# The other order of a block's projections, and scores within 32 tokens on four strips of partitions

## The chip, the cores and the metric

The kernel runs on one core of one Trainium2 chip. A core has a matrix engine (PE, whose weight loads are listed apart as PEld), a vector engine (DVE), an activation engine (ACT), a general engine (POOL) and a queue engine (SP) that issues the DMA transfers. Each works through a list of its own, in the list's order, and the program has it wait on semaphores where it needs another engine's result. The metric is the device time of the whole program in microseconds (us), lower is better. Times are medians of repeated runs on one chip.

## The reference

One layer of a hybrid backbone over 4096 latent tokens of 1024 channels, with a prefix of 256 context tokens:

```python
a_lat = rmsnorm(h_lat, norm_g) * (1.0 + sc_l) + sh_l
q, zf, zb, v, ga, u, ug, gb = split(a_lat @ w_in)            # 8 groups of 512 columns
f = lb + (1 - lb) * sigmoid(z);  k = 1 - f                   # forget gates, forward and backward
S_t = diag(f_t) S_{t-1} + k_t v_t^T;  o_t = S_t^T q_t        # 4 heads of 128, both directions
y = silu(layernorm(depthwise_conv31(u * sigmoid(ug)) + b))   # half the channels along rows, half along columns
h = h_lat + gt * concat(head_rmsnorm(o) * silu(ga), y * silu(gb)) @ w_out
out = rmsnorm(h)
```

The latent scans of both directions start from the final states of the context. All of it is float32; the kernel takes each float32 projection as three float16 products (a high and a low half of each operand, without low times low).

## The kernel before, in words

A first sweep goes forward over 16 blocks of 256 tokens (two groups of 128), a second one goes backward over the groups. The first sweep does the projections of z (both directions), q, v, u and ug, the forward recurrence, the row convolution, and stores what the second sweep needs. The second sweep does the gates ga and gb, the column convolution, the backward state's term, the norms and the output projection.

Inside a block the recurrence of a group (`hgrn`, L707) is done without a loop over tokens. Two tokens s and t belong to the level h (1, 2, 4, ...) where s xor t lies in [h, 2h). For each level, ACT gathers the decayed keys of both directions into a tile `km` (L743), PE multiplies them with the decayed queries into a PSUM tile `pl` (`scores`, L712 to L719), DVE multiplies the keys and queries in the tile `X` by the forget factors of the next level (L750, L751), and a predicated copy under a mask (L754) puts the level's entries of `pl` into the tile `SD`. Level 0 (`kap`, L730) is the token with itself. Levels 1 to 32 are done within halves of 64 tokens: each product has 64 keys as weights and 64 queries as moving columns, the first half on partitions 0 to 63 of the output, the second on 64 to 127. So a level has 16 products (2 groups, 4 heads, 2 halves), and as float32 each is two weight loads and two matmul instructions (passes). The last level, 64, multiplies one half with the other (L761, L762). After it the keys are split into halves of float16 (`split_keys`: `K` on ACT L554 and DVE L555) and transposed by DMA (`X<-K`, L556); with them PE forms the state's increment `pu` (L572), and with the assembled score tile `SC` (ACT copies, L783, L784) the output `po` (L789, L790).

Beside the recurrence of block b run, side by side, the row convolution of b on DVE (`row_conv`, 62 instructions, L690 and L698), the projections, the norm and transposition of the rows of block b + 2 (`prep_rows`), and in blocks 1 to 10 the preparation of the second sweep's weights. `merge` (L46) issues the steps of these generators at an even pace; then a scheduler of the framework, which works with its own estimates of time, settles the order of each engine's list. In the kernel before, the projections beside block b are in this order: ug and u of block b (`project_uv`), v of block b, then z and q of block b + 1 (`project_fq`). The row convolution needs the product `gu` of u and sigmoid(ug), so its generator first idles for a fifth of its steps.

Tiles come from pools with a fixed number of buffers per tag: `X` has 2 (one per group), `km` 3 (shared with `kap`, `SC` and `sg`), the projections' PSUM tile 2, `gu` three tags in turn.

Of the kernel before, what the change touches and what calls it, by code (L numbers as in the profile page):

```python
# [19 lines left out]
P = 128  # L20
# [12 lines left out]
LEVELS = (1, 2, 4, 8, 16, 32)  # L33
# [3 lines left out]
# row packing of the per-channel vectors  # L37
# [5 lines left out]
def merge(*gens):  # L43
    """Issue the steps of several generators side by side, each at an even pace."""
# [28 lines left out]
def rsqrt(nc, pool, out, v, n, tag, eng=None):  # L73
    """out = v ** -0.5 for [128, n] columns, by Newton's iteration to float32's accuracy."""
# [23 lines left out]
def hymba_block(  # L98
# [47 lines left out]
    def exponent(out_s, out_r, ssq):  # L146
        """From a sum of squares: r = a power of two over sqrt(ssq / 2), s = 2^14 / r."""
# [4 lines left out]
        # the halved biased exponent, taken as a number, is 2^-64 of the power sought  # L152
# [7 lines left out]
    def group_scale(ssq, g):  # L160
        """The scale of a group of columns, from sums of its squares."""
# [14 lines left out]
    def split_chunk(hi, lo, st, g, dve=False):  # L176
        """hi + lo = scale * st, both float16."""
# [10 lines left out]
    # ---------------------------------------------------------------- sweep 1  # L188
    wp = ctx.enter_context(tc.tile_pool(name="wp", bufs=1))
    e1 = ctx.enter_context(tc.tile_pool(name="e1", bufs=1))  # L190
    with ExitStack() as s1:
# [55 lines left out]
        def prep_rows(r0, aT):  # L247
            """The same for later blocks: modulated as rows, and transposed by DMA."""
# [28 lines left out]
        def proj_cm(ps, w, aT, ct):  # L277
            """ps[:, j] = columns ct + j of a group, channels on partitions."""
# [38 lines left out]
        masks = m1.tile([P, len(LEVELS), H], U8, name="masks")  # L317
# [3 lines left out]
        # ---------------------------------------------------------- set-up  # L321
        # Staging of what set-up reads: tiles that the blocks use only later.
# [75 lines left out]
        # per-partition columns of the vectors  # L398
# [4 lines left out]
        # silu(c) as c * sigmoid(c); the softmax of two logits as a sigmoid of their difference  # L403
# [5 lines left out]
        # modulation  # L409
        mcol = const([P, 16, 2], name="mcol")  # L410
        for j in MOD:
# [17 lines left out]
            # four rows of 128 at a time, each on a quarter of the columns  # L429
# [18 lines left out]
        with tc.high_priority():  # L448
# [4 lines left out]
            # a normed row of 1024 has no entry over 32, so a^2 <= 2 (1024 g^2 + sh^2)  # L453
# [747 lines left out]
```

## Time and profile before

| what | us |
|---|---|
| median of 3 runs (2247.38 to 2247.63) | 2247.4 |
| span of the profiled execution, from its first to its last instruction | 2247.5 |
| PE busy | 2134.2 |
| PEld busy | 1678.9 |
| DVE busy | 1795.7 |
| ACT busy | 970.8 |
| POOL busy | 462.2 |

The profiled execution's span and the median of the runs differ by 0.1 us, so the trace may be read as the time itself. Busy time is the union of an engine's instructions; matmuls overlap each other, so the length of a matmul is not what it adds: that is the distance from its start to the next one's start. In the timeline a row stands for a run of equal instructions, with its start, its length and its count; the length contains the last instruction's latency, and the next row's start tells what the run really took. A block of the first sweep is seen best between two copies of line 734, of which there is one per block.

### The profile page before, as it was taken

The numbers are of one execution on the slowest core, as the hardware profiler recorded it, in microseconds if no ns is written. First come the engines' busy times: TensorE is split into PE (matmuls) and PEld (weight loads), VectorE is DVE, ScalarE is ACT, GpSimd is POOL, SyncE is SP. The second block draws the span as 40 slices with busy tenths as digits, with TensorE's granted clock in tenths as the row PEclk, the third lists the DMA queues.
The fourth block names the chain that finished last, engine by engine and source line by source line (L and its number), as shares of the span: only waits on it lengthen the run. The fifth ranks groups of instructions, "written<-read, shape, count | busy, mean of one in ns | idle before, by whom it ended". The sixth has DMA issues, their size and how long they took to land. (4 is left out here: it accounts for less than half of the span.)

```text
span 2247.5 us, 47494 instructions
## 1 busy us (share of the span) xinstructions
PE 2134.2 (95%) x18750; PEld 1678.9 (75%) x18750; DVE 1795.7 (80%) x4288; ACT 970.8 (43%) x2150; POOL 462.2 (21%) x1146
## 2 busy tenths in 40 slices
PE   6999999999998999999999999999899999999997
PEld 3778778778777778778778778686667777667776
DVE  5999887887886987987977976988878888877754
ACT  5944535435535435435435434332433333334333
POOL 1120101001010001001101000034444333443332
PEclk8999999999999999999999999999999999999999
DMA  9425435424425345244223205543233232223332
GB/s 363 130 77 165 127 86 156 97 70 137 102 64 164 79 134 166 65 139 109 60 64 77 57 25 160 157 163 108 94 101 101 90 115 97 90 95 105 108 102 71
DMA packets 221448, 251.19 MB, mean 112 GB/s; under 512 B 143812, under 2 KB 147736, under 8 KB 216744
## 3 DMA queue, kind: packets, MB, share of 16 engines
q1 hardware_dynamic: 220104, 239.67, 36.1%
q0 software_dynamic: 1120, 8.49, 1.0%
q8 instruction: 147, 2.41, 0.5%
q14 instruction: 77, 0.63, 0.1%
HBM read 137.99 MB, written 76.55 MB: 95 GB/s over the span
## 5 line engine op out<-in xcount | busy, mean ns | idle before, releaser
L283 PEld LDWEIGHTS <-w 128*128 128x128 f16 x4704 | 451.2, 98 | 67.9 <-issue 2.6
L698 DVE SCALAR_TENSOR_TENSOR yr<-gu,convw,yr 128x224 f32<-128x224 f32 (+2 forms) x900 | 353.1, 442 | 0.0
L1020 DVE SCALAR_TENSOR_TENSOR ycs<-gu_all,convw,ycs 128x256 f32<-128x256 f32 (+2 forms) x828 | 344.2, 467 | 0.0
L283 PEld LDWEIGHTS <-pair 128*128 128x128 f16 x3168 | 308.9, 98 | 36.7
L1118 PE MATMUL py<-wo,yh 128*128 128x512 f32 x1024 | 277.7, 410 | 3.5 <-ACT yh L1102 3.4
L80 POOL TENSOR_SCALAR xqh<-xssq 128x1 f32<-128x1 f32 x30 | 14.9, 498 | 1056.5 <-DVE xssq L256 1056.5
L743 ACT COPY km<-X 128x512 f32<-128x512 f32 x192 | 126.5, 665 | 239.9 <-DVE X L751 236.7
L1118 PEld LDWEIGHTS py<-wo,yh 128*128 128x128 f32 x1024 | 187.3, 190 | 43.3 <-ACT yh L1102 4.4
L987 PE MATMUL ps_gb<-aT,w 128*128 128x256 f16 x1536 | 190.4, 273 | 0.0
L283 PE MATMUL ps_z<-aT,w 128*128 128x256 f16 x1632 | 186.9, 274 | 1.9 <-DVE aT L241 1.4
L294 PE MATMUL pv<-w,aT 128*128 128x512 f16 x816 | 184.1, 379 | 0.1
L975 PE MATMUL ps_ga<-w,aT 128*128 128x512 f16 x768 | 180.2, 387 | 3.5 <-DMA aT<-aTd 3.5
L283 PE MATMUL ps_u<-aT,w 128*128 128x256 f16 x1536 | 182.8, 274 | 0.0
L283 PE MATMUL ps_z<-aT,pair 128*128 128x256 f16 x1632 | 182.7, 273 | 0.0
L283 PE MATMUL ps_g<-aT,w 128*128 128x256 f16 x1536 | 180.8, 273 | 0.0
L283 PE MATMUL ps_q<-aT,pair 128*128 128x256 f16 x1536 | 180.7, 274 | 0.0
L987 PEld LDWEIGHTS <-w 128*128 128x128 f16 x1536 | 146.2, 98 | 31.4 <-issue 15.1
L294 PEld LDWEIGHTS <-aT 128*128 128x128 f16 x816 | 77.5, 98 | 88.3 <-issue 0.8
L975 PEld LDWEIGHTS <-aT 128*128 128x128 f16 x768 | 73.3, 99 | 93.8 <-issue 13.7
L1118 PE MATMUL py<-wo,yl 128*128 128x512 f32 x512 | 138.8, 399 | 0.0
L718 PEld LDWEIGHTS pl<-X,km 128*64 128x64 f32 x3072 | 106.2, 138 | 38.5 <-issue 28.0
L718 PE MATMUL pl<-X,km 128*64 128x64 f32 x3072 | 126.8, 232 | 4.4 <-ACT km L743 4.3
(266 smaller groups left out, 3394.5 us busy)
## 6 DMA issues: line engine op xcount, KB each, us to landing
xt<-in_x_dram SPq DMA_DIRECT2D x64, 512.0 KB, 3.7
out_dram<-xt SPq DMA_DIRECT2D x31, 512.0 KB, 2.6
aTd<-aT SPq DMA_DIRECT2D x14, 1024.0 KB, 7.4
aT<-aTd SPq DMA_DIRECT2D x14, 1024.0 KB, 5.3
wst<-in_w_in_dram SPq DMA_DIRECT2D x16, 512.0 KB, 4.4
wod<-hl SPq DMA_DIRECT2D x32, 256.0 KB, 3.5
qbd<-X SPq DMA_DIRECT2D x31, 256.0 KB, 2.2
ubd<-ub SPq DMA_DIRECT2D x31, 256.0 KB, 2.3
```

Source lines behind the costliest of these rows:

```text
L80: eng.tensor_scalar(h, v, -0.5, 0.0, ALU.mult, ALU.add)
L283: nc.tensor.matmul(ps[:, j, :], w[:, wi, k, (ct + j) * P : (ct + j + 1) * P], aT[:, ai, k, :], start=n == 0, stop=n == 23)
L294: nc.tensor.matmul(pv, aT[:, ai, k, i * P : (i + 1) * P], W[G_V][:, wi, k, :], start=n == 0, stop=n == 23)
L698: nc.vector.scalar_tensor_tensor(ar[i][:, :, lo:hi], gr[i][:, :, lo + dl : hi + dl], convw[:, i, j : j + 1], ar[i][:, :, lo:hi], ALU.mult, ...
L718: nc.tensor.matmul(pl[t0 : t0 + H, gi, hd, :], keys[gi][:, hd, t0 : t0 + H], queries(gi, hd, t0), start=True, stop=True)
L743: nc.scalar.copy(fap(km, 0, kd), fap(Xs[gi], 0, ks))
L975: nc.tensor.matmul(ps, aT[:, ai, k, i * P : (i + 1) * P], Wa[:, wi, k, :], start=n == 0, stop=n == 23)
L987: nc.tensor.matmul(ps[:, j, :], Wb[:, wi, k, (ct + j) * P : (ct + j + 1) * P], aT[:, ai, k, :], start=n == 0, stop=n == 23)
L1020: nc.vector.scalar_tensor_tensor(ya, gu_all[:, i, (lo + dl) * GW : (hi + dl) * GW], convw[:, 2 + i, j : j + 1], ya, ALU.mult, ALU.add)
L1118: nc.tensor.matmul(py, y[:, k // 4, k % 4, :], W2[wi, nh][:, k, :], start=n == 0, stop=n == 23)
```

## The change

The levels that are done within a stretch of tokens now end at 16 (`LEVELS`), and the stretch is Q = 32 tokens: a product has 32 keys and 32 queries, four of them stand on the four strips of 32 partitions of a `pl` tile of half the size, and a level has 32 products. `SD` and the masks are half as large. Level 32 becomes a product of one stretch with its neighbour (`across(Q)`, 32 products), level 64 stays a product of one half with the other (`across(H)`, 16 products). The score tile `SC` is put together in more copies: 8 of 32 partitions and 2 of 64 per group instead of 4 of 64.

The order of the projections beside block b becomes: v of block b, z and q of block b + 1, then ug and u of block b + 1 (`project_gu`, `project_v`). So `gu` of a block is there when the block starts, and its convolution starts without idling. `gu` of block 0 is made in the set-up, that of block 15 in its own block. The sigmoid is written into `gu` itself and no longer into a `km` buffer. Three tiles of the last block are allocated later.

```diff
-LEVELS = (1, 2, 4, 8, 16, 32)
+LEVELS = (1, 2, 4, 8, 16)
+Q = 32
...
-        def project_uv(b, aT, d):
+        def project_gu(b, aT, d):
             for ct in (0, 2):
+                if b == NB - 1 and ct == 2:
+                    gu = late["gu"][:, :, b * TB : (b + 1) * TB]
+                else:
+                    gu = e1.tile([P, 2, TB], F32, tag=f"gu{(2 * b + ct // 2) % 3}", name="gu")
                 ps = ps_pr.tile([P, 2, TB], F32, tag="pr", name="ps_g")
                 yield from proj_cm(ps, W[G_UG], aT, ct)
-                sg = m1.tile([P, 2, TB], F32, tag="km", name="sg", bufs=3)
-                nc.scalar.activation(sg, ps, AF.Sigmoid, scale=es[:, 0, G_UG : G_UG + 1])
+                nc.scalar.activation(gu, ps, AF.Sigmoid, scale=es[:, 0, G_UG : G_UG + 1])
...
+        N_GU = 8
+
+        def project_v(aT, d):
...
             def scores(keys, queries):
-                pl = ps_lv.tile([P, 2, NH, H], F32, tag="lv", name="pl")
+                pl = ps_lv.tile([P, 2, NH, Q], F32, tag="lv", name="pl")
                 for gi in range(2):
                     for hd in range(NH):
-                        for t0 in (0, H):
-                            nc.tensor.matmul(pl[t0 : t0 + H, gi, hd, :], keys[gi][:, hd, t0 : t0 + H], queries(gi, hd, t0), start=True, stop=True)
+                        for t0 in range(0, P, Q):
+                            nc.tensor.matmul(pl[t0 : t0 + Q, gi, hd, :], keys[gi][:, hd, t0 : t0 + Q], queries(gi, hd, t0), start=True, stop=True)
                 return pl
...
+            def across(h):
+                pl = ps_lv.tile([P, 2, NH, h], F32, tag="lv", name="pl")
+                for gi in range(2):
+                    for hd in range(NH):
+                        for t0 in range(0, P, 2 * h):
+                            lo, hi = slice(hd * P + t0, hd * P + t0 + h), slice(hd * P + t0 + h, hd * P + t0 + 2 * h)
+                            nc.tensor.matmul(pl[t0 : t0 + h, gi, hd, :], Xs[gi][:, 0, lo], Xs[gi][:, 2, hi], start=True, stop=True)
+                            nc.tensor.matmul(pl[t0 + h : t0 + 2 * h, gi, hd, :], Xs[gi][:, 3, hi], Xs[gi][:, 1, lo], start=True, stop=True)
+                return pl
+
+            SCs = []
+            pl = across(Q)
+            for gi in range(2):
+                SC = m1.tile([P, NH, P], F32, tag="km", name="SC", bufs=3)
+                for t0 in range(0, P, Q):
+                    t1 = t0 ^ Q
+                    nc.scalar.copy(SC[t0 : t0 + Q, :, t1 : t1 + Q], pl[t0 : t0 + Q, gi])
+                    nc.scalar.copy(SC[t0 : t0 + Q, :, t0 : t0 + Q], SD[t0 : t0 + Q, gi])
+                SCs.append(SC)
+                grow(gi, Q)
+                yield
+            pl = across(H)
...
-            gens = [(N_HGRN, hgrn(b, d)), (N_CONV * 5 // 4, chain(idle(N_CONV // 4), row_conv(b, d)))]
-            proj = [project_uv(b, aTs[b], d)]
-            n_proj = N_UV
+            gens = [(N_HGRN, hgrn(b, d)), (N_CONV * 5 // 4, chain(idle(N_CONV // 4 if late_gu else 0), row_conv(b, d)))]
+            proj = [project_gu(b, aTs[b], d)] if late_gu else []
+            proj.append(project_v(aTs[b], d))
             if b + 1 < NB:
                 proj.append(project_fq(aTs[b + 1], blk[b + 1]))
-                n_proj += N_FQ
-            else:
-                n_proj *= 2
-            gens.append((n_proj, chain(*proj)))
+            if b + 2 < NB:
+                proj.append(project_gu(b + 1, aTs[b + 1], blk[b + 1]))
+            gens.append((2 * N_UV if late_gu else N_V + N_FQ + N_GU, chain(*proj)))
```

The engines' lists move with it. The first place is the end of block 5 in DVE's list. `X<-X,FL` are the multiplications of the last level, `K` the low halves of the keys (which the DMA transposes wait for), `yr` the row convolution, `xt` and `hl` the rows of a later block. Before:

```order
L766 TENSOR_TENSOR X<-X,FL 128x8x64
L767 TENSOR_TENSOR X<-X,FL 128x8x64
L698 SCALAR_TENSOR_TENSOR yr<-gu,convw,yr 128x4x53
L267 TENSOR_TENSOR hl<-xt,hl 128x512
L698 SCALAR_TENSOR_TENSOR yr<-gu,convw,yr 128x4x53
L267 TENSOR_TENSOR hl<-xt,hl 128x512
L555 SCALAR_TENSOR_TENSOR K<-X,K 128x512
L698 SCALAR_TENSOR_TENSOR yr<-gu,convw,yr 128x4x52
L555 SCALAR_TENSOR_TENSOR K<-X,K 128x512
```

With the change, from the first group's last multiplications on:

```order
L768 TENSOR_TENSOR X<-X,FL 128x8x64
L769 TENSOR_TENSOR X<-X,FL 128x8x64
L263 SCALAR_TENSOR_TENSOR xt<-xt,xr,gs 128x512 x2
L768 TENSOR_TENSOR X<-X,FL 128x8x64
L769 TENSOR_TENSOR X<-X,FL 128x8x64
L265 TENSOR_TENSOR xt<-xt,gs 128x512
L556 SCALAR_TENSOR_TENSOR K<-X,K 128x512
L265 TENSOR_TENSOR xt<-xt,gs 128x512
L556 SCALAR_TENSOR_TENSOR K<-X,K 128x512
```

The convolution has left the end of the block. It stands at the front now: the second place is the same list from block 5's second `kap` to the multiplications of level 1 (`gu` is the second half of the next gated input, `v` the low half of the values). Before:

```order
L730 TENSOR_TENSOR kap<-X 128x512
L267 TENSOR_TENSOR hl<-xt,hl 128x512
L750 TENSOR_TENSOR X<-X,f 128x512
L751 TENSOR_TENSOR X<-X,f 128x512
L670 SCALAR_TENSOR_TENSOR gu<-ps_u,es,sg 128x512
```

With the change, the last part of what stands between them:

```order
L807 COPY fb_all<-FL 128x4
L706 SCALAR_TENSOR_TENSOR yr<-gu,convw,yr 128x4x63 x4
L706 SCALAR_TENSOR_TENSOR yr<-gu,convw,yr 128x4x62
L564 SCALAR_TENSOR_TENSOR v_8680<-v,v_8680 128x512
L706 SCALAR_TENSOR_TENSOR yr<-gu,convw,yr 128x4x62
L706 SCALAR_TENSOR_TENSOR yr<-gu,convw,yr 128x4x61 x2
L706 SCALAR_TENSOR_TENSOR yr<-gu,convw,yr 128x4x60 x2
L758 TENSOR_TENSOR X<-X,f 128x512
L759 TENSOR_TENSOR X<-X,f 128x512
```

From the second `kap` to level 1 there are now 18 instructions of the convolution, one of `gu` and one of `v`, where one of `hl` stood. The third place is SP's list in block 14, at the loads of the columns for the second sweep (`gu_all`) and of its weights (`w_7`). Before, the key transposes `X<-K` of the block stand ahead of all 15 column loads:

```order
L556 DMA_TRANSPOSE X<-K 128x8x128 x2
L702 DMA yrd_218<-yr 128x512
L556 DMA_TRANSPOSE X<-K 128x8x128 x2
L795 DMA opd_136<-osb 128x512
L804 DMA ubd_200<-ub 128x512
L795 DMA opd_137<-osb 128x512
L804 DMA ubd_201<-ub 128x512
L901 DMA gu_all<-gud_234 128x2x256
```

With the change, from the first group's transposes on:

```order
L557 DMA_TRANSPOSE X<-K 128x8x128 x2
L931 DMA gu_all<-gud_228 128x2x256
L931 DMA gu_all<-gud_227 128x2x256
L931 DMA gu_all<-gud_226 128x2x256
L931 DMA gu_all<-gud_225 128x2x256
L931 DMA gu_all<-gud_224 128x2x256
L931 DMA gu_all<-gud_223 128x2x256
L931 DMA gu_all<-gud_222 128x2x256
L557 DMA_TRANSPOSE X<-K 128x8x128 x2
```

Six column loads stand ahead of the first transposes now, seven between the two pairs. On PE, where a level's products stood in the first levels as two runs of 8 products, every level is one run of 32; in block 5, 103 matmuls of 256 columns stood between level 64 and the first `pu`, and 81 stand there now.

## Rows read from the trace of the kernel before

**Rows 1.** The page: busy time of each engine, share of the span, instructions.
```profile
PE 2134.2 (95%) x18750; PEld 1678.9 (75%) x18750; DVE 1795.7 (80%) x4288; ACT 970.8 (43%) x2150; POOL 462.2 (21%) x1146
```

**Rows 2.** Windows of the blocks' stretch and of block 5: length, busy time by engine, clock.
```profile
122.00:1455.00 1333.00, 1281.57 (x13615) 1040.97 (x13613) 1104.22 (x2465) 599.92 (x1167) 122.33 (x198) 0.99 0.39 106
...
531.00:614.00 83.00, 80.36 (x870) 65.99 (x868) 70.15 (x153) 39.52 (x77) 9.14 (x14) 1.00 0.37 105
```

**Rows 3.** Source line 734, once per block: duration, first and last start.
```profile
L734 ACT COPY SD<-pl x16: 580/585/586, 130.7 to 1393.0; 128x512 f32<-128x512 f32 x16
```

**Rows 4.** Timeline of PE in block 5: start, length, instruction, count, idle before.
```profile
549.71 0.85 PE L718 MATMUL pl<-X,km 128*64 128x64 f32 x16
550.49 2.58 PE L283 MATMUL ps_u<-aT,w 128*128 128x256 f16 x22
...
572.28 6.00 PE L294 MATMUL pv<-w,aT 128*128 128x512 f16 x27
578.21 1.15 PE L718 MATMUL pl<-X,km 128*64 128x64 f32 x32
579.29 0.60 PE L294 MATMUL pv<-w,aT 128*128 128x512 f16 x2
...
592.58 10.65 PE L283 MATMUL ps_z<-aT,pair 128*128 128x256 f16 x96
603.07 0.93 PE L283 MATMUL ps_q<-aT,pair 128*128 128x256 f16 x7
605.60 0.83 PE L572 MATMUL pu<-v,X 128*128 128x128 f16 x12 [1.60 <-DMA X<-K]
606.26 0.44 PE L789 MATMUL po<-v,SC 128*128 128x128 f32 x2
...
608.11 2.78 PE L283 MATMUL ps_q<-aT,pair 128*128 128x256 f16 x24
```

**Rows 5.** Waits of PE between 122 and 1455 us: total us, times, longest.
```profile
PE pu L572 <- DMA X<-K: 22.9, 14, 2.5
...
PE pl L718 <- ACT km L743: 4.3, 8, 1.3
```

**Rows 6.** Source line 433 and timeline: products on four strips of 32 columns.
```profile
L433 PE MATMUL pm<-w,sc x32: 1033/1061/1063, 7.0 to 20.6; 128*32 128x512 f32 x32
...
10.06 1.94 PE L433 MATMUL pm<-w,sc 128*32 128x512 f32 x8 [1.15 <-DMA w<-in_w_mod_dram]
```

**Rows 7.** Timeline of DVE at the end of block 5.
```profile
592.46 1.41 DVE L262 SCALAR_TENSOR_TENSOR xt<-xt,xr,gs 128x512 f32<-128x512 f32 x2 [1.33 <-POOL xr L84]
593.79 0.80 DVE L698 SCALAR_TENSOR_TENSOR yr<-gu,convw,yr 128x220 f32<-128x220 f32 x2
...
596.07 0.68 DVE L766 TENSOR_TENSOR X<-X,FL 128x512 f32<-128x512 f32 x1
596.67 0.68 DVE L767 TENSOR_TENSOR X<-X,FL 128x512 f32<-128x512 f32 x1
...
600.73 0.67 DVE L555 SCALAR_TENSOR_TENSOR K<-X,K 128x512 f16<-128x512 f32 x1
```

**Rows 8.** Timeline of SP, the DMA queue, in the same stretch.
```profile
598.93 3.13 SPq L270 DMA_TRANSPOSE aT<-hl  x2
602.17 1.28 SPq L556 DMA_TRANSPOSE X<-K  x1
```

**Rows 9.** The page's costliest groups: busy us, mean ns, idle before.
```profile
L698 DVE SCALAR_TENSOR_TENSOR yr<-gu,convw,yr 128x224 f32<-128x224 f32 (+2 forms) x900 | 353.1, 442 | 0.0
...
L743 ACT COPY km<-X 128x512 f32<-128x512 f32 x192 | 126.5, 665 | 239.9 <-DVE X L751 236.7
```

**Rows 10.** Groups by form: predicated copies into SD.
```profile
L754 DVE COPY_PREDICATED SD<-masks,pl 128x512 f32<-128x512 uint8 x96 | 69.5, 724 | 0.0
```

**Rows 11.** Source lines 901 and 556: issue times, and landing of the key transposes.
```profile
L901 SPq DMA_DIRECT2D gu_all<-gud x15: 550/610/1418, 1384.1 to 1394.1; - x15
...
DMA to landing us min/median/max: 3.1/3.3/10.3
```

More of the change, by code (lines that the diff above doesn't have):

```diff
@@ L680, in project_uv @@
                 d["v"].append(v)
-        N_UV = 12
+        N_V = 4
+        N_UV = N_V + N_GU
         def row_conv(b, d):
             gu = d["gu"]
+            if b == NB - 1:
+                late["yc"] = e1.tile([P, 4, TB], F32, tag="A", name="yc15")
             acc = late["yc"][:, 0:2, :] if b == NB - 1 else m1.tile([P, 2, TB], F32, tag="yr", name="yr")
@@ L744, in hgrn @@
                     kms.append(km)
-                qs = [[2 * h, H // (2 * h)], [S + h, 2]] + ([[1, h]] if h > 1 else [])
+                qs = [[2 * h, Q // (2 * h)], [S + h, 2]] + ([[1, h]] if h > 1 else [])
                 pl = scores(kms, lambda gi, hd, t0: fap(Xs[gi], S + hd * P + t0, qs))
@@ L753, in hgrn, with grow @@
                     if gi == 1:
-                        nc.vector.copy_predicated(SD, fap(masks, li * H, [[0, 2 * NH], [1, H]]), pl)
+                        nc.vector.copy_predicated(SD, fap(masks, li * Q, [[0, 2 * NH], [1, Q]]), pl)
                     yield
-            h = H
-            pl = ps_lv.tile([P, 2, NH, H], F32, tag="lv", name="pl")
-            for gi in range(2):
-                for hd in range(NH):
-                    lo, hi = slice(hd * P, hd * P + H), slice(hd * P + H, hd * P + P)
-                    nc.tensor.matmul(pl[0:H, gi, hd, :], Xs[gi][:, 0, lo], Xs[gi][:, 2, hi], start=True, stop=True)
-                    nc.tensor.matmul(pl[H:P, gi, hd, :], Xs[gi][:, 3, hi], Xs[gi][:, 1, lo], start=True, stop=True)
-            for gi in range(2):
-                f, X, FL, g = fts[gi], Xs[gi], FLs[gi], 2 * b + gi
+            def grow(gi, h):
+                f, X, FL = fts[gi], Xs[gi], FLs[gi]
                 xa, xb = xhalf(X, h, 0, 0, S, 2), xhalf(X, h, 1, 2, S, 2)
@@ L768, in hgrn @@
                 double_f(f, FL, h)
+            def across(h):
[17 more added lines that the diff above has]
+                grow(gi, Q)
+                yield
+            pl = across(H)
+            for gi in range(2):
+                X, FL, g = Xs[gi], FLs[gi], 2 * b + gi
+                for t0 in (0, H):
+                    nc.scalar.copy(SCs[gi][t0 : t0 + H, :, H - t0 : P - t0], pl[t0 : t0 + H, gi])
+                grow(gi, H)
                 for dirn in (1, 0) if b == NB - 1 and gi else (0, 1):
@@ L771, in hgrn @@
                 if b == NB - 1 and gi:
+                    late["qu"] = e1.tile([P, 2, NH, P], F32, tag="xt", name="qu", bufs=2)
                     nc.scalar.copy(late["qu"][:, 0].rearrange("p h t -> p (h t)"), X[:, 1, :])
@@ L779, in forward @@
             def forward(gi, V):
-                X, v, g = Xs[gi], d["v"][gi], 2 * b + gi
-                SC = m1.tile([P, NH, P], F32, tag="km", name="SC", bufs=3)
-                for t0 in (0, H):
-                    nc.scalar.copy(SC[t0 : t0 + H, :, t0 : t0 + H], SD[t0 : t0 + H, gi])
-                    nc.scalar.copy(SC[t0 : t0 + H, :, H - t0 : P - t0], pl[t0 : t0 + H, gi])
+                X, v, g, SC = Xs[gi], d["v"][gi], 2 * b + gi, SCs[gi]
                 pu = keys_to_u(X, V, 0)
@@ L791, in forward @@
                 update(s_f, FLs[gi][:, 0, 504:508], pu)
+                if last and gi == 0:
+                    late["op"] = e1.tile([P, 2, NH, P], F32, tag="xt", name="op", bufs=2)
                 osb = late["op"][:, gi] if last else m1.tile([P, NH, P], F32, tag="ub", name="osb", bufs=2)
```

36 lines of the change are left out of this document (17 added, 19 removed).

## The prediction

> **What bounds the kernel now.** First the busy times: PE is busy for 2134.2 of 2247.5 us [rows 1]. The stretch of the 16 blocks, 122 to 1455 us, is where the change lies; there PE is busy for 1281.57 of 1333.00 us, so idle for 51.4 us, at a granted clock of 0.99, so nearly all of it at the 2.4 GHz level [rows 2]. One block lasts (1393.0 - 130.7) / 15 = 84.2 us [rows 3]. The second sweep keeps its work, and I count its change as nothing.
>
> Then PE's timeline of a clean block [rows 4], read by distances between starts. 96 matmuls of 256 columns take 603.07 - 592.58 = 10.49 us; a block has 480 of them: 52.5. Of the 512-column ones, 27 take 578.21 - 572.28 = 5.93, so 48 take 10.5. The 12 of `pu` take 0.66, four times: 2.6. The 16 passes of `po` take 608.11 - 606.26 = 1.85, twice: 3.7. A level as one run of 32 passes takes 579.29 - 578.21 = 1.08, a half run 550.49 - 549.71 = 0.78. Block 5 has three levels as half runs and five as whole ones, so 5 x 1.08 and 6 halves between 0.54 and 0.78, put at 0.67: 9.4. The sum is 78.7. Against 84.2 there are 5.5 us a block that aren't work: 51.4 us of idleness over 15.8 blocks is 3.2, the rest is the latency at the switches between kinds of product and the short stretches at half clock.
>
> Who ends the idleness: PE's largest wait by far is `pu` for the DMA of the transposed keys, 22.9 us, of which 1.60 lie before the `pu` at 605.60; waits of the levels' products for `km` are only 4.3 us [rows 4, 5]. So PE's work is the bound, and the keys at a block's end are the second one. DVE is busy for 70.15 of block 5's 83.00 us, ACT for 39.52 [rows 2]: DVE has 13 us of room in a block, but not everywhere.
>
> **The change part by part.** *PE's products.* Before: 9.4 us a block. After: seven runs of 64 passes of 32 columns (`kap`, levels 1 to 16, `across(Q)`), and level 64 as before. What such a pass costs isn't in the trace. The nearest rows: a pass of 128 columns takes 1.85 / 16 = 0.116 us; of 64 columns, two strips of which run at a time, 32 passes take 1.08, so 16 rounds of 0.059 and about 0.14 at the ends. Per column that is the same price, so a round of 32 columns is put at about 0.031. That four strips run side by side is seen in the set-up: 8 float32 passes with 32 columns of weights, each 1.061 us long, are done in 1.94 us, so in two rounds of four [rows 6]. Then a run has 64 / 4 = 16 rounds: 16 x 0.031 + 0.14 = 0.64. From the other side: if a pass costs its 1.08 / 32 = 0.034 whatever its columns and strips, a run takes 64 x 0.034 = 2.16. Between them: two strips of 64 and four of 32 take the same, 1.08. The row of four strips is nearest in form, but its passes are long, and a run of 64 short ones has to be fed; I take 0.70. After: 7 x 0.70 + 1.08 = 6.0, a gain of 3.4 us a block, 55 us over 16. Ends: 5.6 (a gain of 61), 8.6 (of 12), and 16.2 (a loss of 109).
>
> The page "TensorEngine Tiling (Array Packing)" of the Trainium skill (section Instruction Overhead) speaks against this: each matmul has an overhead of about 60 cycles, and a tiling factor is not to be taken from a dimension that is already small. By it, read as paid pass after pass at 2.4 GHz, a pass would not fall under 25 ns, an estimate, and a run would take 64 x 0.025 + 0.14 = 1.74 us. The trace has four strips side by side, and has no pass of under 64 columns in a long run; so that stays a rival below.
>
> *The end of a block.* In block 5 level 64 ends on PE at 592.58 and `pu` starts at 605.60: 13.0 us, bridged by 103 matmuls (11.3 us). DVE's list has the convolution between the multiplications and the keys' low halves, and SP issues `aT<-hl` for 3.13 us ahead of `X<-K` [rows 7, 8]. Now only 81 matmuls (81 x 0.109 = 8.9 us) bridge it, but the chain is shorter: four multiplications at 596.67 - 596.07 = 0.60 each, two of `xt` in 593.79 - 592.46 = 1.33, one more `xt` and one `K` at 0.60 are 4.9 us, and the transposes land 3.3 us after their issue [rows 7, 11], with `aT<-hl` no longer ahead. 8.3 against 8.9: no wait left, with half a microsecond to spare. I leave 0.5 us of the 3.2 for scatter.
>
> *The front of a block.* The convolution (62 instructions a block, 353.1 / 900 = 0.39 each [rows 9]) now stands before level 1's multiplications. From the second `kap` to their end DVE has 18 of these (7.1), `gu` and `v` (1.3), small ones (0.7), four multiplications and one more of the convolution (2.8): 11.9, and 0.67 for `km` on ACT, 12.5 in all until level 2's product may start. PE needs 0.7 + 12 x 0.22 + 0.7 + 2.6 + 24 x 0.109 = 9.2 for what it has before that product. DVE is ahead by some 2.6 us when it makes the second `kap`: after the last `pu` PE still has 21 x 0.109 + 24 x 0.22 = 7.6 us, and DVE and ACT need about 5 with what stands between. So a new wait of 0.7 us there, and perhaps 0.5 at each of the next levels, where 9 and 6 of the convolution stand beside 5.9 us of PE's work: 2 us a block. With the 0.5 above, 2.5 stand for the old 3.2: a gain of 0.7 a block, 11 us. Bounds: none of the waits left (51 us gained), or DVE not ahead at all, 2.6 us more a block (42 lost).
>
> *Other edits.* A predicated copy is half as wide and there is one fewer, 69.5 / 96 = 0.72 each [rows 10]: 2.4 us of DVE less a block, which I have used nowhere but in the front's room. ACT gets twelve more small copies for `SC` and loses two `km` of 0.67 [rows 9] and half of `SD`; about 1 us more in a block where it idles for 43, at nothing; without that room it would delay the keys by that 1 us. `gu` written over its sigmoid: at nothing, since its buffer was last read by a convolution that is now early. `gu` of block 0 moves to the set-up, its 192 matmuls are only done sooner.
>
> *Block 14, once.* On SP six column loads stand ahead of the first `X<-K` and seven between the two pairs, 0.61 us each to issue, and the loads share the DMA engines with the transposes, which landed in up to 10.3 us [rows 11]. The first six start when q is done, before level 64; the seven cost 4.3 us. I take 5 us, from 0 to 12.
>
> **Sum.** 2247.5 - 55 - 11 + 7 (5 for block 14, 2 for the seams to the set-up and to the second sweep) = 2188. The span is 0.1 us over the median of the runs, so it holds for these too.
>
> **The rivals.**
> A, the forecast: 2188, chance 0.58.
> B, the strips give nothing: four strips of 32 take as long as two of 64, since weights and columns are as many per run. For it: no run in the trace has four strips of short passes. Against it: rows 6. Then 2247.5 - 12 - 11 + 7 = 2232. Chance 0.14.
> C, the other side: PE pays by the pass, not by the column. Place: the seven runs of a level. Price 2.16 instead of 1.08 us, 16.2 for 9.4 a block: 2247.5 + 109 - 11 + 7 = 2352. It turns the change into a loss from about 1.2 us a run. For it: twice as many passes and loads, in runs twice as long as any before. Against it: passes of two strips start close together already, else 32 of them would not fit into 1.08 us. By the page's overhead the seven runs take 12.2 and the block's products 13.3, an estimate, and the time is 2247.5 + 62 - 4 = 2306. Chance 0.08.
> D, DVE's crowded front becomes the bound: `kap` comes late as well, and each block waits 2.6 us more for `km`: 2188 + 42 = 2230. For it: ACT's `km` already waits 236.7 us for DVE's multiplications [rows 9]. Against it: DVE has 13 us of room and loses 2.4 of work. Chance 0.13.
> E, all waits of the blocks vanish, since the keys and the convolution no longer meet: 2247.5 - 55 - 51 + 7 = 2148. Chance 0.07.
>
> **How the numbers follow.** The time is that of A. A's own range is 2165 to 2215. For 8 in 10 I go down to E's 2150 and up past B and D to 2240; C and the outer half of E are left out. 0.2% of the time is 4.5 us, about what a measurement of this kernel tells from no change. Faster: all of A and E, most of B and D, 0.85. Same: what of B and D comes out some 12 us worse, 0.06. Slower: C and the ends of D, 0.09.
>
> **What would show it.** A run of 64 passes `pl` takes 0.6 to 0.8 us by starts: right; 1.08 is B, over 1.2 is C. The distance between two `SD` copies falls from 84.2 to about 80. PE's waits at `pu` fall under 10 us in all, outside block 14; waits of `pl` for `km` rise from 4.3 to about 30 us (over 70 is D). In block 14 one wait of a few us stands before a `pu`. If the time is under 2150 or over 2240, a price here is wrong by more than its bounds suggest: first the run of passes, then the front of the block.

## The result and the profile after

The changed kernel takes 2215.6 us (median of four runs, 2215.1 to 2218.5) beside 2247.5 for the kernel before on the same chip: a ratio of 0.985, 95% interval 0.984 to 0.987. That is 32 us faster, where 59 were forecast; the time lies in the range (2150 to 2240) and just above A's own (2165 to 2215). The profiled execution lasts 2215.8 us with a span of 2214.0. The page's busy times, to be read beside [rows 1]:

```profile
PE 2083.6 (94%) x22334; PEld 1642.5 (74%) x22334; DVE 1749.6 (79%) x4270; ACT 996.3 (45%) x2310; POOL 458.5 (21%) x1146
```

PE has 51 us less to do and 3600 instructions more. The windows, cut at the first `kap` of a block on DVE, tell where the time went (columns as in [rows 2]). First the kernel before: block 0, blocks 1 to 10, blocks 11 to 13.

```profile
122.10:198.40 76.30, 74.40 (x809) 59.76 (x807) 71.02 (x162) 36.22 (x72) 9.66 (x14) 1.00 0.44 118
198.40:1048.10 849.70, 808.43 (x8612) 661.74 (x8610) 711.20 (x1578) 397.06 (x774) 89.20 (x147) 0.99 0.42 115
...
1048.10:1294.70 246.60, 239.57 (x2572) 196.58 (x2570) 196.67 (x445) 107.85 (x214) 22.30 (x35) 0.99 0.27 65
```

The same stretches of the changed kernel:

```profile
128.90:213.90 85.00, 77.99 (x1089) 63.52 (x1087) 77.39 (x172) 37.25 (x81) 7.68 (x11) 0.98 0.47 122
213.90:1042.40 828.50, 782.99 (x10883) 643.42 (x10882) 674.43 (x1560) 412.30 (x874) 88.53 (x147) 0.98 0.41 115
...
1042.40:1270.70 228.30, 228.13 (x3269) 188.97 (x3267) 188.32 (x441) 112.74 (x245) 21.24 (x35) 1.00 0.29 69
```

Three stretches behave differently. In blocks 11 to 13 PE is never idle (228.13 of 228.30 us) and a block takes 76.1 us instead of 82.2: 6 us gained, more than forecast. In blocks 1 to 10, where the second sweep's weights are prepared on the side (ACT and DVE do that work in blocks 1 to 9), a block takes 82.9 instead of 85.0, and PE is idle for 45.5 us where it was for 41.3. So a block with the preparation was 2.8 us longer than one without it, and is 6.8 us longer now. And the start is later: the first `kap` comes at 128.9 instead of 122.1 and block 0 takes 85.0 instead of 76.3. By stage, with the forecast's terms spread over them (4.1 us a block; 5 for block 14; 2 for the seams; us, negative is shorter):

| stage | forecast | measured |
|---|---|---|
| set-up and block 0 | -3 | +15.5 |
| blocks 1 to 10 | -41 | -21.2 |
| blocks 11 to 13 | -12 | -18.3 |
| block 14 | +1 | -2.1 |
| block 15 and second sweep | -3 | -7.4 |
| sum | -58 | -33.5 |

The `SD` copies, which answer to [rows 3]: (1360.5 - 145.2) / 15 = 81.0 us a block, from 84.2.

```profile
L742 ACT COPY SD<-pl x16: 357/364/376, 145.2 to 1360.5; 128x256 f32<-128x256 f32 x16
```

A run of 64 passes, in PE's timeline (start, length, count), which answers to [rows 4]:

```profile
557.98 0.38 PE L295 MATMUL pv<-w,aT 128*128 128x512 f16 x1
558.29 0.76 PE L726 MATMUL pl<-q,kap 128*32 128x32 f32 x64
558.99 0.39 PE L295 MATMUL pv<-w,aT 128*128 128x512 f16 x1
```

It takes 558.99 - 558.29 = 0.70 us. In blocks 1, 12 and 13 all products `pl` together take 6.08. PE's waits from 122 to 1430 us, beside [rows 5] (total, times, longest):

```profile
PE pu L573 <- DMA X<-K: 27.3, 12, 4.6
PE pl L726 <- ACT km L751: 19.2, 23, 1.6
```

Beside these, [rows 5] leave out two rows of the kernel before:

```profile
PE pu L572 <- DVE xssq L256: 7.5, 3, 2.9
PE pu L572 <- DVE hl L881: 4.4, 2, 2.3
```

These five waits before `pu` are put down to DVE, but they end 3.4 us after the issue of `X<-K`, as most of those put down to the DMA do. So the waits for the keys were 34.8 us, not 22.9. They have fallen to 27.3, and not gone. Where they come from is read at the end of block 4 on DVE, to be set beside [rows 7] (`hl<-wst` are the low halves of later weights, `A` is the buffer that `hl` lies in):

```profile
506.43 0.43 DVE L762 COPY_PREDICATED SD<-masks,pl 128x256 f32<-128x256 uint8 x1
508.47 1.28 DVE L184 SCALAR_TENSOR_TENSOR hl<-wst,rwall,hl 128x1024 f16<-128x1024 f32 x1 [1.61 <-ACT hl L183]
515.23 1.28 DVE L184 SCALAR_TENSOR_TENSOR hl<-wst,rwall,hl 128x1024 f16<-128x1024 f32 x1 [5.48 <-ACT hl L183]
...
520.66 0.15 DVE L257 TENSOR_SCALAR xssq<-xssq 128x1 f32<-128x1 f32 x1 [1.74 <-ACT hl L256]
...
524.44 1.42 DVE L263 SCALAR_TENSOR_TENSOR xt<-xt,xr,gs 128x512 f32<-128x512 f32 x2 [2.24 <-POOL xr L85]
525.77 0.69 DVE L768 TENSOR_TENSOR X<-X,FL 128x512 f32<-128x512 f32 x1
...
527.58 0.68 DVE L556 SCALAR_TENSOR_TENSOR K<-X,K 128x512 f16<-128x512 f32 x1
```

Behind the last level's copy DVE waits four times, 11.1 us in all, with the levels' multiplications and the keys queued behind. ACT's rows say for what: each low half waits for its high half, and that waits until a DMA has read out the buffer `A`, which the rows use too; the row's square waits for it as well.

```profile
507.29 1.15 ACT L183 ACTIVATE hl<-wst,rwall 128x1024 f16<-128x1024 f32 x1 [1.91 <-DMA aT<-hl]
...
514.05 1.15 ACT L183 ACTIVATE hl<-wst,rwall 128x1024 f16<-128x1024 f32 x1 [2.11 <-DMA w2d<-hl]
...
519.48 1.06 ACT L256 ACTIVATE hl<-xt 128x1024 bf16<-128x1024 f32 x1 [0.42 <-DMA w2d<-hl]
```

So the low half of the keys is made at 527.58, 8.1 us after level 64's last product on PE; SP issues the transposes then, and PE waits 3.08:

```profile
528.34 2.60 SPq L557 DMA_TRANSPOSE X<-K  x2
```

PE's row for `pu`:

```profile
531.69 1.44 PE L573 MATMUL pu<-v,X 128*128 128x128 f16 x12 [3.08 <-DMA X<-K]
```

It starts 3.4 us after the issue, as in the kernel before, so the transposes were not slower here. The twelve `pu` then take 1.23 us by starts instead of 0.66: with five of the twelve waits the granted clock is at half for 3.4 or 6.8 us, and in blocks 1 to 10 for 34 us in all, where it was for 17 before. Block 12 has no preparation. There the rows `xt` were done earlier, nothing stands between multiplications and keys, and the low half comes 2.2 us after the product:

```profile
1178.53 0.68 DVE L768 TENSOR_TENSOR X<-X,FL 128x512 f32<-128x512 f32 x1
1179.13 0.68 DVE L769 TENSOR_TENSOR X<-X,FL 128x512 f32<-128x512 f32 x1
1179.74 1.49 DVE L556 SCALAR_TENSOR_TENSOR K<-X,K 128x512 f16<-128x512 f32 x2
```

### The profile page after: what moved, and what is told of

Read it like the earlier page. It is cut to its first block, busy times and chain, and to the rows that moved or that the text cites. A ratio compares the mean times of both kernels' runs of the same rounds, so it can differ in the third digit from the quotient of the medians.

```text
span 2214.0 us, 54678 instructions
## 1 busy us (share of the span) xinstructions
PE 2083.6 (94%) x22334; PEld 1642.5 (74%) x22334; DVE 1749.6 (79%) x4270; ACT 996.3 (45%) x2310; POOL 458.5 (21%) x1146
## 5 line engine op out<-in xcount | busy, mean ns | idle before, releaser
L284 PE MATMUL ps_z<-aT,pair 128*128 128x256 f16 x1632 | 191.1, 277 | 0.0
L751 ACT COPY km<-X 128x512 f32<-128x512 f32 x160 | 107.9, 675 | 168.2 <-DVE X L759 167.9
L284 PE MATMUL ps_q<-aT,pair 128*128 128x256 f16 x1536 | 172.9, 273 | 0.0
L314 ACT ACTIVATE f<-f,lbv,oml 128x128 f32<-128x128 f32 x272 | 113.0, 485 | 0.1
L1146 PEld LDWEIGHTS py<-wo,yl 128*128 128x128 f32 x512 | 95.0, 192 | 19.1
```

What stands on the lines that cost most here:

```text
L284: nc.tensor.matmul(ps[:, j, :], w[:, wi, k, (ct + j) * P : (ct + j + 1) * P], aT[:, ai, k, :], start=n == 0, stop=n == 23)
L314: nc.scalar.activation(fa, fa, AF.Identity, scale=oml[:, d, ct + j : ct + j + 1], bias=lbv[:, d, ct + j : ct + j + 1])
L751: nc.scalar.copy(fap(km, 0, kd), fap(Xs[gi], 0, ks))
L1146: nc.tensor.matmul(py, y[:, k // 4, k % 4, :], W2[wi, nh][:, k, :], start=n == 0, stop=n == 23)
```

## The experiments

Two profiles of the changed kernel itself differ by 8 us in blocks 3 to 10 (661 and 653), so only larger differences there are read. Ratios are to the kernel before on the same chip; `pu` is the total of PE's waits before `pu` that are put down to `X<-K`, up to 1430 us of the span, the lengths of blocks are by the first `kap` on DVE.

| kernel | median us | ratio, 95% | blocks 3 to 10 | pu |
|---|---|---|---|---|
| before | 2247.5 | | 685 | 22.9 |
| changed | 2215.6 | 0.985 (0.984 to 0.987) | 661 | 27.3 |
| e1 strips only | 2218.5 | 0.986 (0.984 to 0.988) | 671 | 26.2 |
| e2 order only | 2239.2 | 0.995 (0.994 to 0.997) | 664 | 23.6 |
| e3 rows behind keys | 2215.2 | 0.984 (0.981 to 0.987) | 657 | 19.6 |
| e4 no preparation | 2155.9 | 0.958 (0.956 to 0.960) | 610 | 4.5 |
| e5 changed, again | 2212.8 | 0.985 (0.984 to 0.987) | 653 | 24.7 |
| e6 preparation behind keys | 2221.6 | 0.989 (0.987 to 0.990) | 660 | 6.8 |
| e7 preparation on POOL | 2228.9 | 0.993 (0.991 to 0.994) | 676 | 20.1 |
| e8 buffer of its own | 2218.3 | 0.986 (0.984 to 0.988) | 661 | 24.8 |
| e9 e8, loads by POOL | 2235.5 | 0.992 (0.990 to 0.995) | 664 | 37.5 |
| e10 halves before keys | 2238.8 | 0.995 (0.993 to 0.997) | 689 | 42.1 |
| e11 work without waits | 2172.9 | 0.965 (0.962 to 0.968) | 624 | 4.0 |
| e12 moves without work | 2245.8 | 0.998 (0.996 to 0.999) | 689 | 46.2 |

**e1 and e2: the two parts alone.** e1 puts the old order back, e2 the old scores.

```diff
 e1
-        fq0 = chain(project_fq(aTs[0], blk[0]), project_gu(0, aTs[0], blk[0]))
+        fq0 = project_fq(aTs[0], blk[0])
...
-            proj = [project_gu(b, aTs[b], d)] if late_gu else []
+            proj = [project_gu(b, aTs[b], d)]
...
-            if b + 2 < NB:
-                proj.append(project_gu(b + 1, aTs[b + 1], blk[b + 1]))
 e2
-LEVELS = (1, 2, 4, 8, 16)
-Q = 32
+LEVELS = (1, 2, 4, 8, 16, 32)
+Q = 64
...
```

> The new scores on four strips, with the old order of the projections (values and gated inputs of a block beside its own levels, the convolution idling a quarter first). If the strips alone carry the gain, a block's products take 6.0 us instead of 9.4 and the waits stay as they were (3.2 us a block): 2247.5 - 55 = 2193. If PE only comes sooner to the same wait (the keys' chain at the end of a block, with the convolution and aT<-hl in front, is as long as before, and 3.4 us less of PE work lie in the block), part of it turns into waits at pu, 22.9 -> 40 to 60 us: 2210 to 2230.

> The new order of the projections, with the old scores on two strips (six levels of 64 columns, 9.4 us of products a block). By the prediction's terms: -11 for waits, +7 for block 14 and the seams: 2243. By what the changed kernel's trace shows (waits at pu fall from 43 to 29 us in the blocks, new waits for km of 25): between 2243 and 2255, no gain by itself. If the order is the larger part of the measured gain: under 2230.

The strips alone give as much as both, the second of e1's two expectations: besides 26.2 us of waits at `pu` for `X<-K`, 23 more before `pu` are put down to DVE, and 20.4 of these end 3.4 us after the issue of `X<-K` too. The order alone gives 11 us where its own terms had 4; its profiled run is the slowest of ten. Together the order adds nothing that the intervals could tell. The profiles say why: beside e1, the changed kernel is 11.7 us faster in blocks 11 to 13 and 8.8 in blocks 1 to 10, but its block 0 ends 20.2 us later (213.9 against 193.7). Up to block 1's first `kap` PE has 160 more matmuls of 256 columns to do there than in e1, 135 of ug and u and 25 of q, 17.5 us at 0.109 us each, and is idle for some 3.7 us longer. From block 15's `kap` on it has 181 fewer (135 and 46), 19.7 us, yet only 4.8 us less than in e1 are needed: PE waits at the seam between the sweeps, and runs at half clock there. PE's timeline there, and then a window (clock 0.51).

```profile
1438.00 1.05 PE L1078 MATMUL pi<-s_b,qb 128*128 128x128 f32 x8
1448.92 2.04 PE L1078 MATMUL pi<-s_b,qb 128*128 128x128 f32 x8 [9.87 <-DMA qb<-qbd]
```

The window:

```profile
1442.00:1459.00 17.00, 7.62 (x25) 6.19 (x26) 14.59 (x39) 5.90 (x19) 7.87 (x24) 0.51 0.52 190
```

**e3: the rows behind the keys.** `after(x)` puts an instruction behind `x` in its engine's list; `marks["K"]` is the last low half of the keys.

```diff
+            keys = marks["K"]
...
+            marks["K"] = nc.vector.scalar_tensor_tensor(K[:, 1, :], kx, 2.0 ** 14, K[:, 0, :], ALU.mult, ALU.subtract)
...
-                    nc.vector.scalar_tensor_tensor(ts, ts, r, gs[:, 0, sl], ALU.mult, ALU.mult)
+                    with after(keys): nc.vector.scalar_tensor_tensor(ts, ts, r, gs[:, 0, sl], ALU.mult, ALU.mult)
```

> The changed kernel, but on DVE the multiplications of a later block's rows (xt) are queued behind the four low halves of the keys; the same work, another order. Theory 1 (in the blocks with weight preparation DVE's list puts rows, which wait 2.24 us for POOL, between the last multiplications and the keys' low halves, so X<-K comes 5 us late): in blocks 4 and 5 the low half comes 2.5 to 4 us after level 64's last product instead of 8.1, their waits at pu (3.4 each) fall under 0.5, in all 27.3 -> about 18 us; with the half clock that follows a wait the time is 2200 to 2208. Rival (SP's list and the landing of the transposes set the wait): pu keeps its waits, 2215. Rival (DVE has too much to do in these blocks, whatever the order): the wait goes to the front, pl for km, and the time stays within 2212 to 2218.

In blocks 4 and 5 it did what theory 1 said: the low half comes 3.9 us after the product instead of 8.2, the waits are 0.8 and 0.9 us instead of 3.1 and 3.2. In all `pu` fell to 19.6, the waits for `km` rose from 19.2 to 23.1, and the time is the same as e5's within the intervals, not the 2200 to 2208 of theory 1. The chain is shown; that it costs time is not.

**e4: no preparation.** The generators of `side` only store resident data to the same places.

> The changed kernel without the preparation of the second sweep's weights in blocks 1 to 10: their halves, the gate row's products and the output projection's factors are left out, and copies of other resident data are stored in their place, so the second sweep computes with other numbers at the same shapes. Theory 1 and the rival of DVE's load both expect blocks 1 to 10 to run like blocks 11 to 13 (76 us instead of 78.5 to 88) and waits at pu only in blocks 0 and 14 (3 to 6 us in all): 2215 - 65 = 2150. If SP's list and the landings set the wait, pu keeps 15 us or more of its 27.3 and the time stays over 2185.

Blocks 3 to 10 run at 76.2 us, and PE is idle for only 1.7 us in blocks 1 to 10 (first row):

```profile
214.80:976.00 761.20, 759.50 (x10877) 628.83 (x10875) 643.84 (x1492) 381.78 (x830) 77.43 (x140) 1.00 0.32 85
366.10:976.00 609.90, 608.20 (x8707) 503.50 (x8706) 515.31 (x1194) 305.34 (x664) 61.73 (x112) 1.00 0.32 85
```

So the preparation costs the changed kernel 67 us in blocks 1 to 10 (828.5 against 761.2), though it gives DVE only 30.6 us of work there (674.43 - 643.84), and DVE idles for 117 us of these blocks without it (761.2 - 643.8). Of the 67 us, 44 are idleness of PE; the rest is a longer busy time (783.0 against 759.5), at a granted clock of 0.98 instead of 1.00. In the kernel before, blocks 1 to 10 were 28 us longer than ten like blocks 11 to 13. So the preparation costs more than twice as much now, and that is where the forecast's gain went. e5 to e12 ask what it is of the preparation that costs.

**e5 and e6: the low halves behind the keys as well.** e6 is e3 with two more edits of this kind:

```diff
-            split_chunk(hl[:, 0, :], hl[:, 1, :], t, g)
+            with after(marks["K"]): split_chunk(hl[:, 0, :], hl[:, 1, :], t, g)
...
-                    nc.vector.tensor_tensor(w, w, gw[:, 0, :], ALU.mult)
+                    with after(marks["K"]): nc.vector.tensor_tensor(w, w, gw[:, 0, :], ALU.mult)
```

> The changed kernel as it is, beside the next two on the same chip, to be compared with them and with the kernels of the first four experiments: 2212 to 2220 by every theory.

> As the kernel with the rows behind the keys, and the DVE work of the weight preparation (the low halves, and the products with the gate row) is queued behind the keys of the block before too, so that it lies at the front of its block. The runs so far: without this preparation blocks 1 to 10 take 761 us instead of 829; 22 us of the difference lie before pu, 24 in and before the levels, 7 in po and its half clock. Theory 2 (its instructions cost by where they stand in DVE's and ACT's lists, in front of the keys and between the levels): waits at pu fall from 27.3 to under 10 us, and some of it comes back at the front as later kap: blocks 1 to 10 take 790 to 805, the time is 2185 to 2200. Rival (DVE's and ACT's added load, or the sharing of the row buffers, costs the same wherever it stands): blocks 1 to 10 stay at 820 or more, 2208 to 2220.

e6 cleared the end of every block from 3 to 10: the low half comes 2.24 us after the product, as in block 12. The blocks are no shorter. PE's waits of e6:

```profile
PE pl L726 <- ACT km L751: 33.0, 35, 1.8
PE pu L573 <- DMA X<-K: 6.8, 6, 3.3
```

The wait has moved to the front: 20 us less before `pu` for the keys, 14 more at `km`, 8 more before `pu` for `v` and `osb`, 3 more for `gu`. DVE now waits 1.1 to 3.9 us for ACT before a block's last low half of the weights, and does rows beside the convolution. The rival's time, 2208 to 2220, was just passed (2221.6). Theory 2 fell in its price: the lists decide where PE waits, not how much.

**e7: the preparation on POOL.**

```diff
-            split_chunk(hl[:, 0, :], hl[:, 1, :], t, g)
+            nc.gpsimd.tensor_scalar(t, t, rwall[:, g, 0:1], None, ALU.mult); nc.gpsimd.tensor_copy(hl[:, 0, :], t); nc.gpsimd.tensor_tensor(hl[:, 1, :], t, hl[:, 0, :], ALU.subtract)
...
-                nc.scalar.copy(hl[:, 0, :], w)
+                nc.gpsimd.tensor_copy(hl[:, 0, :], w)
```

> The changed kernel with the halves of the later weights and their products with the gate row computed on POOL instead of ACT and DVE; the shared buffers (xt, A) stay shared, and are held longer if POOL is slower. Theory 2 (the cost is the place in DVE's and ACT's lists): blocks 3 to 10 run at 76 to 78 us, the time is 2160 to 2175. Rival (the cost is the shared buffer A, which is held for some 12 us in the middle of a block and moves the rows to the block's end): nothing is gained or it gets worse, 2210 to 2235. Rival (POOL's own use of memory slows DVE while it runs): DVE's mean time of a multiplication of a level rises above its 0.60 us, and part of the gain is lost, 2180 to 2205.

The second expectation held: 16 us slower than e5 with work taken off DVE and ACT. A part of 1024 columns takes POOL 3.2 + 1.0 + 2.1 us (medians) where ACT and DVE need 1.15 and 1.28, and in block 4 `A` is held for some 23 us by the two parts, 12 in the changed kernel. DVE's multiplications keep their 0.68 us, so the third expectation is out.

**e8 to e10: a buffer of its own.** The halves go to 2 KB of their own in smaller pieces (e8); the squares too, and POOL issues the loads of `gu_all` (e9); DVE's part is held between the levels and the last multiplications (e10).

```diff
 e8
-            hl = e1.tile([P, 2, 2 * 512], F16, tag="A", name="hl")
+            for n in range(2):
+                hl = e1.tile([P, 2, 512], F16, tag="A2", name="hl")
...
 e9
-                nc.sync.dma_start(late["gu"][:, :, b * TB : (b + 1) * TB], gud[b])
+                nc.gpsimd.dma_start(late["gu"][:, :, b * TB : (b + 1) * TB], gud[b])
 e10
-                grow(gi, H)
+                with after(marks["side"]): grow(gi, H)
```

> The changed kernel; the halves of the later weights are written to a buffer of 2 KB of their own, in pieces of half the size, instead of to the rows' buffer A (the same work on the same engines, 2 KB of the set-up's staging moved to yr). Theory 3 (the place decides: a low half or a row that waits in DVE's list for a buffer, for ACT or for POOL holds up the level or the keys behind it, and PE never gets that back; in blocks without the preparation the rows lie where DVE waits for PE anyway, at 46 to 55 us of the block): with A free the rows go back to that place, the low halves need 2.6 to 5.5 us of DVE a block in its 10.7 us of idleness: waits at pu 27.3 -> under 12, those for km 19 -> under 15, blocks 1 to 10 take 785 to 800 instead of 821 to 829, the time is 2180 to 2192. Rival (DVE's and ACT's added load is what costs, wherever it lies): blocks 1 to 10 stay over 815, 2205 to 2220.

> As the kernel before it in this list, and: the squares for the scales in block 2 also go to the new buffer, and the column loads of gu_all in blocks 14 and 15 are issued by POOL instead of SP. If SP's column loads in front of X<-K cost the 1.4 to 1.6 us of the wait at pu in block 14, that wait goes; with block 2 it is another 2 to 8 us: 2175 to 2190. If the landings and not SP's issuing are late there, nothing changes in block 14, and only block 2 gains, 0 to 4 us.

> The kernel with the buffer of its own for the later weights' halves; in blocks 3 to 10 the preparation is now issued after the rows of its own block, and on DVE it is held between the predicated copy of a level and the last multiplications of the block (it may not start before the one, and these may not start before it is done), so nothing but the four low halves stands between the multiplications and X<-K, and nothing new stands at the front. The four kernels before kept the same work at the front (pu waits gone, front waits up), on POOL, or left the halves in the tail; none gained. Theory 3 (the place decides): in blocks 3 to 9 the low half of the keys comes 2.2 to 3 us after level 64's last product, waits at pu there are under 0.5, blocks 1 to 10 take 795 to 808, the time is 2188 to 2200. Rival (DVE has no place left in a block of 76 us for 2.6 to 6 us more; each us added costs PE about a us wherever it lies): the waits turn up before level 32 and 64 (pl for X or km), blocks 1 to 10 take 815 or more, 2207 to 2225.

None gained: e8 has the rival's time, e9 is 17 us slower than e8, and e10 is slower than even its rival (2207 to 2225). In e8 most rows went back to 51 to 58 us of a block (51 to 56 in e4), as theory 3 said, but pieces of the halves now stood at the end of the block and waited there for loads and for ACT. In e10 the halves stood where they were meant to, and waited there, because the one new buffer had to be stored between two pieces:

```profile
595.31 0.75 DVE L184 SCALAR_TENSOR_TENSOR hl<-wst,rwall,hl 128x512 f16<-128x512 f32 x1 [3.62 <-ACT hl L183]
601.43 0.75 DVE L184 SCALAR_TENSOR_TENSOR hl<-wst,rwall,hl 128x512 f16<-128x512 f32 x1 [3.81 <-ACT hl L183]
```

ACT's row for the first of them:

```profile
594.56 0.72 ACT L183 ACTIVATE hl<-wst,rwall 128x512 f16<-128x512 f32 x1 [3.46 <-DMA w2d<-hl]
```

So these runs tell that my placements were bad, not what the work costs. For block 14 e9 tells only that the loads are worse on POOL: the wait there is 12.8 us, 1.3 in e8. The changed kernel's own SP row there tells more:

```profile
1333.64 4.85 SPq L557 DMA_TRANSPOSE X<-K  x2
```

The first pair is issued 4.3 us after level 64's last product, 3.0 in block 12, behind the column loads; the issue takes 4.85 us, 2.60 in block 4. So SP's list costs 1.3 us there, and the transposes are slower as well.

**e11 and e12: the work and the waits, each without the other.** e11 computes the halves and products from resident data, at the place of e10; e12 moves the weights through `xt` and `A` by DMA, with no ACT or DVE work.

```diff
 e11
+                h = e1.tile([P, 2, 512], F16, tag="A2", name="h")
+                with after(marks["lev"]): marks["side"] = split_chunk(h[:, 0, :], h[:, 1, :], st, G_V)
...
 e12
+            hl = e1.tile([P, 2 * 512], F32, tag="A", name="hl")
...
+            nc.sync.dma_start(hl, t)
+            nc.sync.dma_start(jd[g][i], hl)
```

> As the kernel without the preparation of the later weights (76 us a block), but in blocks 3 to 10 ACT and DVE compute as much as that preparation does, from resident data and into a buffer that waits for no DMA: in blocks 3 to 6 four pairs of an ACT copy and a DVE low half of 512 columns, in blocks 7 to 10 four products, four copies and four differences of 512 columns; on DVE they lie between the predicated copies and the last multiplications of a block. No weights are loaded or stored for it, and the second sweep again computes with other numbers. Blocks 3 to 10 took 661 us in the changed kernel and 610 without the preparation. Theory 4 (what costs is the waiting of instructions in DVE's list for buffers, loads and stores, and the rows that are pushed to the end of the block; DVE's work itself fits into its 10 us of idleness): 612 to 625 us, the time 2157 to 2172. Rival (each us more on DVE costs PE about a us, wherever it lies; 8 blocks with 2.6 to 5.6 us): 635 to 645, the time 2182 to 2195.

> As the kernel without the preparation, but in blocks 3 to 10 the later weights are loaded into the rows' staging (xt), moved by a DMA into the rows' buffer A and stored from it, as the preparation did, with no ACT or DVE work for it; the second sweep computes with other numbers. Theory 4: the rows of the block after next are pushed behind the last multiplications again, as in the changed kernel, and the keys come late: waits at pu of 1 to 3 us in blocks 3 to 9, blocks 3 to 10 take 635 to 650 us instead of 610, the time is 2180 to 2195. Rival (DVE's and ACT's work is what costs): 610 to 618, 2155 to 2163.

The window of blocks 3 to 10 of e11:

```profile
368.20:992.30 624.10, 612.80 (x8709) 505.45 (x8707) 542.72 (x1244) 322.76 (x695) 72.38 (x112) 0.99 0.31 83
```

And of e12:

```profile
377.90:1066.80 688.90, 628.76 (x8706) 519.23 (x8704) 512.99 (x1195) 308.56 (x664) 85.42 (x112) 0.97 0.43 125
```

The work alone costs 14 us over e4, of the changed kernel's 51: 1 us in blocks 3 to 6, where DVE has four low halves more in each, and 13 in blocks 7 to 10, where it has eight products and differences; there PE waits 8.8 us at `km`. That is within theory 4's range for the blocks, and its time at the end of that range (2172.9). The buffers alone, with DVE busy for no longer than in e4, cost 79: far over both expectations (theory 4 had 635 to 650 us, not 689). In DVE's timeline of block 4 of e12 the same chain as in the changed kernel is seen, with nothing of the preparation in DVE's list:

```profile
529.66 0.15 DVE L257 TENSOR_SCALAR xssq<-xssq 128x1 f32<-128x1 f32 x1 [8.88 <-ACT hl L256]
...
534.47 1.42 DVE L263 SCALAR_TENSOR_TENSOR xt<-xt,xr,gs 128x512 f32<-128x512 f32 x2 [2.07 <-POOL xr L85]
535.80 1.29 DVE L556 SCALAR_TENSOR_TENSOR K<-X,K 128x512 f16<-128x512 f32 x2
```

In blocks 3 to 5, where the side work is low halves but for one product, the changed kernel needs 16 us more than e4, the work alone 1, the buffers alone 30. So there theory 4's direction is shown, though not its size: in e12 a row's square waits 8.88 us for `A`, in the changed kernel 1.74. From block 6 on it is shown less cleanly: in e12 SP's stores `jd<-hl` waited ahead of `X<-K` in blocks 6 to 9 and put off its issue by 4 to 7 us, which the real preparation does by some 0.4, so e12's 79 us is an upper bound. That the 37 us left (51 - 14) are waits for buffers and loads is argued by subtraction and not shown. For it speaks that e10 and e11, with the same kind of work at the same place, differ by 65 us in blocks 3 to 10 (689 and 624); but e10 also moves the rows. No kernel that does the whole computation is faster than the changed one beyond the intervals. Whether the halves would cost as little as in e11 with two full buffers of their own was not tried.

## Why the prediction was right or wrong

**PE's products: right.** 0.70 us a run and 6.0 a block were forecast, 0.70 and 6.08 measured. Rivals B (1.08) and C (2.16) are out. Of the rule in the Trainium skill, page "TensorEngine Tiling (Array Packing)", section Instruction Overhead, the forecast had worked out 1.74 us a run; 64 passes in 0.70 us are 11 ns each, so on four strips the trace does not agree with it as read pass after pass.

**The waits of a block: the step that failed.** "8.3 against 8.9: no wait left, with half a microsecond to spare" priced each instruction by its length and put no wait between them, although [rows 7] show DVE waiting 1.33 us for POOL before two `xt` like those that the new list puts into that chain. In block 4 the chain took from 519.5 to 531.7, where `pu` starts, with 1.74 and 2.24 us of waiting in it. And it generalised block 5, with half of a microsecond, to all blocks: in blocks 10 to 13 `pu` starts 7 us after the product and never waits; outside block 14 it waited 25.3 us in all, not under 10. The chain alone was not the price, though: e6 cleared it in blocks 3 to 10, and they were no shorter. What failed is the term of 2.5 us of waits a block for all blocks alike. PE is idle for 45.5 us in blocks 1 to 10, beside more half clock, and for 0.2 in blocks 11 to 13. e4 shows that the preparation of the weights makes this difference, which the forecast did not price. Rival E holds for blocks 11 to 13, none of the cases for blocks 1 to 10.

**The front: the direction right, the size too large.** About 30 us of waits for `km` were forecast over all blocks, 19.2 measured, against 4.3 before [rows 5]; D's 70 are far. Blocks 11 to 13 have none, so the convolution before level 1 is not their cause there; e4 leaves 2.4 us of them in all.

**"`gu` of block 0 moves to the set-up, its 192 matmuls are only done sooner", at nothing but the seams' 2 us: failed.** Beside e1, 160 matmuls more stand before block 1 (135 of ug and u, 25 of q), and their 17.5 us are late in full: block 1 starts 20.2 us later than in e1. Of the 19.7 us that the end saves, 4.8 are gained; PE waits 9.9 us at the seam and runs at half clock.

**Block 14: the term was mis-sized.** 5 us were forecast; the two waits there are 2.0 us in all, where 1.2 stood before, and the block is 2.1 us shorter than before. The reason given, SP's list and slower transposes, is seen in the trace, at a smaller price.

**ACT at nothing: not refuted.** ACT is busy for 45%; only one wait of PE, 3.4 us, is put down to an `SC` copy, in block 2.

By the table of stages 25 us are missing in all: 18.5 at the start and 20 in blocks 1 to 10, less 14 by which the other stages came out better than forecast. That the time lies in the range owes something to luck: these misses partly cancel, and the range reached up to 2240 for B and D, which did not come.

## What to carry to other kernels

Before a wait is priced away, ask in which stages of the loop the picture was taken: here one block stood for two kinds, and side work with 3 us of DVE a block cost 7 us. Where it could be taken apart (blocks 3 to 5), the work itself cost next to nothing, and its instructions waited in an ordered list for a shared buffer that a DMA had to read out. A chain between engines is priced with the waits that the old trace already shows in it, not by the lengths of its instructions. And work that a new order moves to the front is a cost there if PE is the bound; it comes back at the end only if nothing else is late there.

## What the runs showed of the hardware

Float32 passes of 32 columns on four strips start 11 ns apart on average over a run of 64, where 32 passes on two strips took 34 ns each [rows 4]. In block 14 column loads issued by POOL held up key transposes issued by SP: in e9 the issue of one took up to 8.9 us and the landing up to 9.4, against 3.2 and 6.0 in the changed kernel. With five of the twelve waits before `pu` in the changed kernel (2.9 to 4.7 us) the granted clock went to half, 1.2 GHz, for 3.4 or 6.8 us, with one of 3.2 us in block 5 it did not; at the seam, in the wait of 9.9 us, for 17.
